# The weight sums of a seven-product down projection: one moved from a DMA to VectorE, another to the second pass, and two units of weights prepared before the last convolution

## The chip, the cores and the metric

One core of a Trainium2 chip runs the whole layer. The metric is the device time of one execution in microseconds (us). The kernel before was timed three times: 950.35 us is the median, 949.29 the lowest and 952.23 the highest. One execution was also profiled; its trace is what the text reads.

## The reference

The program is one layer of a diffusion backbone over 512 tokens of width 1024: a token mixer (spatial gating and gated linear attention) and then a channel mixer. The change lies in the last product of the channel mixer, with the two halves of the up projection called `a` and `val`:

```python
a, val = _split(h @ w_up, (D_FF, D_FF))                      # D_FF = 2816
img = a.reshape(bsz, rows, length // rows, D_FF)
a = lax.conv_general_dilated(img, conv_w[:, :, None, :], (1, 1), 'SAME', ...) + conv_b   # 3 x 3, depthwise
return (jax.nn.gelu(a.reshape(bsz, length, D_FF), approximate=False) * val) @ w_down     # (512, 2816) @ (2816, 1024)
```

The result is scaled by `g2x`, added to the residual stream, and normalised.

## The kernel before, in words

**Up projection and convolution.** The 2816 channels are 22 tiles of 128, numbered by `f`. For each `f` TensorE makes two products of 24 matmuls each (`pa` for `a`, `pv` for `val`, both 128 channels x 512 tokens). Every fp32 operand is split into a high and a low part, so that a product is three matmuls per tile of the contraction: `wh`/`wl` are the parts of a weight, `h2h`/`h2l` those of the activations. ScalarE casts the high part (L183 or L1247), VectorE subtracts it for the low part (L184 or L1248). `conv_part` then copies `pa` out of PSUM on ScalarE (L1193), starts the accumulator `cacc` on ScalarE (L1195), adds the other eight taps on VectorE (L1201), applies gelu on ScalarE (L1202) and multiplies by `pv` on VectorE (L1203). That last multiplication is what frees the PSUM bank of `pv`. After every second `f` four half-width operations on VectorE (L1184 to L1187, `token_sums`) build the sums of token halves.

**Down projection.** Two channel tiles make a pair `p` (0 to 10). The product is done with seven block products instead of eight, in two passes. The first pass has a unit `x` for each pair (weights `ra`: the 1024 columns of the even tile, the second 512 with the first 512 added to them; 12 matmuls) and, for each group of two pairs, a unit `t3` (weights `b22`) and a unit `t2` (weights `t2`), 12 matmuls each. With two pairs a group is thus 48 matmuls. The second pass has a unit `rb` for each pair and a unit `t4` for each group, whose weights are the tile `t2` again with one more addend. Activations are split too: `e` and `s` in the first pass (`eh`, `el`, `sh`, `sl` in the trace), `o` and `s` in the second (L270 on ScalarE, L271 on VectorE). Matmuls of the down projection are L1297. They add up in eight PSUM banks: `p1` and `p5` in pool `gl`, `p7` and `p6` in pool `mm`. The two banks of `p6`, the accumulators of `t2`, are the banks that held `pa` and `pv` of the last `f`.

**Weight sums.** Three kinds of sum over blocks of `w_down` are made by accumulating DMAs that GpSimd issues (`accum_op=ALU.add`, queue q0): a block that already lies in SBUF gets another block of HBM added to it, 256 KB each. L1230 does it for the second half of `ra`, L1225 for `b22`, L1275 for `t2` once unit `t2` has split it. A fourth sum, `t2 = ra[0] + b22`, is VectorE's (L1261).

**What sets the order.** `d_raw` issues the plain load of a tile from SyncE (L1228 for `ra` and `rb`, 512 KB; L1224 for `b22`, 256 KB), and `d_load` does so in the order `ra` 0, `b22` 0, `ra` 1, and so on. `ra`, `rb` and the up projection's weights share one ring of four buffers named `raw`, so a load waits until the tile four places earlier has been read by its last reader; for an `ra` that is the sum L1261 and the split. `wh` and `wl` have rings of five. `b22`, `t2`, `e`, `s`, `o`, the convolution's tiles and `h2` come from one pool of 44 buffers (`heap`). A unit is prepared (`prep`) two units ahead of its matmuls (`LEAD = 2`); a scheduling layer then puts all instructions into one queue per engine, each of which runs strictly in order.

Of the kernel before, what the change touches and what calls it, by code (L numbers as in the profile page):

```python
# [13 lines left out]
ALU = mybir.AluOpType  # L14
# [9 lines left out]
FT = 22  # L24
# [9 lines left out]
def backbone_kernel(  # L34
# [7 lines left out]
    V, A, G, T = nc.vector, nc.scalar, nc.gpsimd, nc.tensor  # L42
# [18 lines left out]
    def late(shape, dt=F32, s="l"):  # L61
        return lp.tile(shape, dt, tag="l", name=nm(s))
# [103 lines left out]
    def stream_load(upto):  # L166
        while pos[0] < min(upto, len(specs)):
            i = pos[0]
            ap, kn, n = specs[i]
            raw = wp.tile([P, kn, n], F32, tag="raw", name=nm("raw"), bufs=4)  # L170
            dma(raw, ap)
            raws[i] = raw
            pos[0] += 1

    def stream_split(upto):
        while pos[1] < min(upto, len(specs)):
            i = pos[1]
            stream_load(i + 1)
            _, kn, n = specs[i]
            raw = raws.pop(i)  # L180
            wh = wp.tile([P, kn, n], F32R, tag="wh", name=nm("wh"))
            wl = wp.tile([P, kn, n], F32R, tag="wl", name=nm("wl"))
            A.copy(wh, raw)  # L183
            V.tensor_tensor(wl, raw, wh.bitcast(F32), op=ALU.subtract)  # L184
            splits[i] = (wh, wl)
            pos[1] += 1

    def weights():
        i = pos[2]
        pos[2] += 1  # L190
        stream_split(i + 2)
        stream_load(i + 1 + AHEAD)
        return splits.pop(i)
# [86 lines left out]
    def prod_cm(ps, w, acts, c0=0, n=512):  # L280
        for k in range(KT):
            prod_k(ps, w, acts, k, c0, n)
# [356 lines left out]
    for d in range(2):  # L639
        t_ = late([P, 4, P], s="pmask")  # L640
# [472 lines left out]
    for t in range(4):  # L1113
        row = []
        for hf in range(2):
            t_ = late([P, 512], s="x1")
# [73 lines left out]
    def conv_part(f, pa, pv):  # L1190
        wcol = lambda tap: ccol[:, tap * FT + f:tap * FT + f + 1]
        a_ = heap([P, 8, GW], s="ca")
        A.copy(a_, pa)  # L1193
        acc = heap([P, 8, GW], s="cacc")
        A.activation(acc, pa, AF.Identity, bias=ccol[:, 198 + f:199 + f], scale=wcol(4))  # L1195
        for tap in (0, 1, 2, 3, 5, 6, 7, 8):
            dy, dx = tap // 3 - 1, tap % 3 - 1
            r0, r1 = max(0, -dy), 8 - max(0, dy)
            c0, c1 = max(0, -dx), GW - max(0, dx)
            o = acc[:, r0:r1, c0:c1]  # L1200
            V.scalar_tensor_tensor(o, a_[:, r0 + dy:r1 + dy, c0 + dx:c1 + dx], wcol(tap), o, op0=ALU.mult, op1=ALU.add)  # L1201
        A.activation(acc, acc, AF.Gelu)  # L1202
        V.tensor_tensor(acc, acc, pv.rearrange("p (r w) -> p r w", w=GW), op=ALU.mult)  # L1203
        gact.append(acc)
        if f % 2:
            token_sums(f // 2)
# [9 lines left out]
    NP = FT // 2  # L1216
    wd = ffn_w_down[0]
    tokens = lambda k: wd[k * P:(k + 1) * P, :]
    dloads, dq = [], {}

    def d_raw(kind, p):
        if kind == "b22":
            t_ = heap([P, 512], s="b22")
            dma(t_, tokens(2 * p + 1)[:, 512:])  # L1224
            G.dma_start(t_, tokens(2 * p)[:, 512:], accum_op=ALU.add)  # L1225
        else:
            t_ = wp.tile([P, 2, 512], F32, tag="raw", name=nm("raw"), bufs=4)
            dma(t_, tokens(2 * p + (kind == "rb")).rearrange("p (a c) -> p a c", c=512))  # L1228
            if kind == "ra":
                G.dma_start(t_[:, 1, :], tokens(2 * p)[:, :512], accum_op=ALU.add)  # L1230
        dq[kind, p] = t_

    for p in range(NP):
# [4 lines left out]
    def d_load(upto):  # L1238
        while dpos[0] < min(upto, len(dloads)):
            d_raw(*dloads[dpos[0]])  # L1240
            dpos[0] += 1

    def d_pair():
        return tuple(wp.tile([P, 2, 512], F32R, tag=tag, name=nm(tag)) for tag in ("wh", "wl"))

    def split_into(wh, wl, raw):
        A.copy(wh, raw)  # L1247
        V.tensor_tensor(wl, raw, wh.bitcast(F32), op=ALU.subtract)  # L1248

    t2, ops = {}, {}  # L1250

    def x_prep(p):

        d_load(2 * p + 7)
        ra, b22 = dq.pop(("ra", p)), dq["b22", p]
        t2[p] = heap([P, 512], s="t2")
        w = d_pair()
        split_into(*w, ra)
        e = split_act(flat(gact[2 * p]), s="e", eng=A.copy)
        s = split_act(s12[p].rearrange("p a c -> p (a c)"), s="s", eng=A.copy)  # L1260
        V.tensor_tensor(t2[p], ra[:, 0, :], b22, op=ALU.add)  # L1261
        ops["a11", p] = [z[:, :256] for z in e]
        ops["s3", p] = [z[:, 256:] for z in e]
        ops["s1", p] = [z[:, :256] for z in s]
        ops["s2", p] = [z[:, 256:] for z in s]
        return w

    def t_prep(kind, ps_):

        w = d_pair()  # L1270
        for j, p in enumerate(ps_):
            src = dq.pop(("b22", p)) if kind == "t3" else t2[p]
            split_into(w[0][:, j, :], w[1][:, j, :], src)
            if kind == "t2":
                G.dma_start(t2[p], tokens(2 * p + 1)[:, :512], accum_op=ALU.add)  # L1275
        return w

    def rb_prep(p):

        d_load(2 * NP + p + 3)  # L1280
        rb = dq.pop(("rb", p))
        w = d_pair()
        split_into(*w, rb)
        o = split_act(flat(gact[2 * p + 1]), s="o", eng=A.copy)
        ops["a12", p] = [z[:, :256] for z in o]
        ops["a22", p] = [z[:, 256:] for z in o]
        if p % 2 == 0:
            n = min(2, NP - p) * 256
            s = split_act(s4[p // 2].rearrange("p a c -> p (a c)")[:, :n], n=n, s="s", eng=A.copy)
            for j in range(n // 256):  # L1290
                ops["s4", p + j] = [z[:, j * 256:(j + 1) * 256] for z in s]
        return w
# [14 lines left out]
    units += [("rb", (p,)) for p in range(groups[-2][0], NP)] + [("t4", g) for g in groups[-2:]]  # L1307
    TAIL = groups[-2][0]
    tw = {}

    def prep(i):
        if i < len(units):
            kind, g = units[i]
            tw[i] = x_prep(g[0]) if kind == "x" else rb_prep(g[0]) if kind == "rb" else t_prep(kind, g)

    for f in range(2, FT):
        pa = mm()
        prod_cm(pa, weights(), h2)
        pv = mm()
        prod_cm(pv, weights(), h2)  # L1320
        if f == FT - 1:
            d_load(7)
        conv_part(f, pa, pv)


# [41 lines left out]
    bank = {}  # L1367
    for name, pool in (("p1", gl), ("p5", gl), ("p7", mm), ("p6", mm)):
        bank[name] = [pool() for _ in range(2)]
    LEAD = 2  # L1370

    def steps_x(i, only=None):
        kind, g = units[i]
# [14 lines left out]
                for t in range(2):  # L1388
                    down(bank[name][t], ops[act, p], t, tw[i], jj if j is None else j, False, True, again=True)

    for i in range(LEAD):
        prep(i)
    for i in range(NX - 3):
        prep(i + LEAD)
        steps_x(i)
        if i == 8:
            for hf in range(2):
                t_ = late([P, 512], s="fng")
# [5 lines left out]
    for i in (x_, t3_, t2_):  # L1404
        prep(i + LEAD)
    steps_x(x_, "p1")
# [25 lines left out]
    for i in range(NX + 2, MAIN):  # L1432
        prep(i + LEAD)
        steps_r(i)
    for i in range(MAIN + LEAD, len(units)):
        prep(i)
# [53 lines left out]
```

## Time and profile before

| what | value |
|---|---|
| median of 3 runs | 950.35 us |
| profiled execution: its time / its span | 950.39 us / 948.7 us |
| mean granted TensorE clock | 0.996 |
| busy share of the span: PE / PEld / DVE / ACT / POOL | 97% / 81% / 74% / 41% / 4% |
| first matmul of the down projection | 828.06 us |
| first matmul of the second pass | 895.08 us |

Times in the trace count from the start of the span. PE is TensorE's matmuls, PEld its weight loads, DVE VectorE, ACT ScalarE, POOL GpSimd, and SPq and POOLq are the queues in which SyncE and GpSimd issue DMAs. A row of the timeline gives the start, the duration, the engine, the line, the operation, output<-input, and in brackets how long the engine sat idle before it and what ended that.

### The profile page before, as it was taken

The page shows a single profiled execution, that of the slowest core. Times are in us where ns is not written, and L with a number is a line of the kernel's source. Part 1 is how long each engine was busy: PE and PEld are TensorE (multiplying, and loading weights), DVE is VectorE, ACT ScalarE, POOL GpSimd, SP SyncE. Part 2 cuts the span into 40 slices and gives each one's busy share as a digit, 9 for nine tenths or more (in the row PEclk, how much of TensorE's full clock was granted, in tenths as well). Part 3 has the DMA queues.
Part 4 walks back from the last instruction along what each step waited for, and adds up shares of the span by engine and source line. Part 5 has one row for each costly group of instructions (what it writes and reads, how often), then busy time and mean ns, then how long its engine had stood idle before and what let it go on. Part 6 is the DMA issues. An engine that isn't in the chain of part 4 may idle for free.

```text
span 948.7 us, 12645 instructions
## 1 busy us (share of the span) xinstructions
PE 921.0 (97%) x4735; PEld 770.2 (81%) x4735; DVE 702.0 (74%) x1248; ACT 390.5 (41%) x669; POOL 42.0 (4%) x67
## 2 busy tenths in 40 slices
PE   6999999999999999999999999999999999999996
PEld 5676898988888888888878888988888888877785
DVE  5557768788699655597664447798888788877897
ACT  5146546567443222223222225543333333445674
POOL 3000000000000000000000000000000001143100
PEclk9999999999999999999999999999999999999999
DMA  9940311132047463683432352333333335599632
GB/s 276 341 129 27 112 46 48 42 112 68 19 137 222 142 206 118 188 277 112 133 111 92 109 182 68 102 98 100 100 88 99 102 90 136 102 259 240 172 111 89
DMA packets 150666, 123.50 MB, mean 130 GB/s; under 512 B 6553, under 2 KB 124645, under 8 KB 150605
## 3 DMA queue, kind: packets, MB, share of 16 engines
q1 hardware_dynamic: 143773, 112.61, 39.1%
q0 software_dynamic: 5104, 8.87, 5.4%
q10 hardware_dynamic: 1728, 1.22, 0.4%
q8 instruction: 37, 0.61, 0.3%
q14 instruction: 24, 0.20, 0.1%
HBM read 120.58 MB, written 2.10 MB: 129 GB/s over the span
## 4 chain that ended last, share of the span: by engine, by line
PE 81%; DVE 7%; DMA 5%; issue 2%; SPq 2%; ACT 2%; POOL 0%; DVEq 0%; POOLq 0%; ACTq 0%
PE mm L278 53%; PE mm L304 5%; PE gl L1297 4%; PE gl L738 3%; PE mm L297 3%; PE mm L1297 3%; DMA raw<-in_ffn_w_down_dram 2%; PE mm L289 1%; PE mm L528 1%; PE gl L304 1%; SPq L215 1%; DMA wa<-in_w_ada_dram 1%; PE mm L842 1%; DVE bc L706 1%; DMA b<-in_ffn_w_down_dram 1%
## 5 line engine op out<-in xcount | busy, mean ns | idle before, releaser
L183 ACT CAST wh<-raw 128x1024 fp32r<-128x1024 f32 x118 | 124.0, 1052 | 303.6 <-PE mm L278 237.4
L184 DVE TENSOR_TENSOR wl<-raw,wh 128x1024 fp32r<-128x1024 f32 x118 | 143.9, 1221 | 76.1 <-ACT wh L183 75.7
L278 PE MATMUL mm<-h2h,wh 128*128 128x512 f32 (+1 forms) x352 | 133.6, 380 | 0.0
L278 PE MATMUL mm<-h2l,wh 128*128 128x512 f32 (+1 forms) x352 | 133.6, 380 | 0.0
L278 PE MATMUL mm<-h2h,wl 128*128 128x512 f32 (+1 forms) x352 | 133.6, 380 | 0.0
L1201 DVE SCALAR_TENSOR_TENSOR cacc<-ca,ccol,cacc 128x441 f32<-128x441 f32 (+2 forms) x176 | 121.8, 695 | 6.7 <-ACT cacc L1195 2.5
L278 PE MATMUL mm<-hxh,wh 128*128 128x512 f32 x296 | 116.5, 394 | 0.0
L278 PE MATMUL mm<-hxh,wl 128*128 128x512 f32 x296 | 115.8, 391 | 0.0
L278 PE MATMUL mm<-hxl,wh 128*128 128x512 f32 x296 | 115.5, 390 | 0.0
L278 PEld LDWEIGHTS mm<-h2h,wl 128*128 128x128 f32 x352 | 66.2, 188 | 12.5
L278 PEld LDWEIGHTS mm<-h2h,wh 128*128 128x128 f32 x352 | 66.2, 188 | 12.5
L278 PEld LDWEIGHTS mm<-h2l,wh 128*128 128x128 f32 x352 | 66.2, 188 | 12.2
L278 PEld LDWEIGHTS mm<-hxh,wl 128*128 128x128 f32 x296 | 55.6, 188 | 11.7 <-issue 0.2
L278 PEld LDWEIGHTS mm<-hxh,wh 128*128 128x128 f32 x296 | 55.6, 188 | 11.6 <-issue 0.5
L278 PEld LDWEIGHTS mm<-hxl,wh 128*128 128x128 f32 x296 | 55.6, 188 | 11.2 <-issue 0.2
L1005 DVE SCALAR_TENSOR_TENSOR acc<-wa,cs,acc 128x512 f32<-128x512 f32 x64 | 45.8, 747 | 4.9 <-DMA wa<-in_w_ada_dram 4.9
L1202 ACT ACTIVATE cacc<-cacc 128x512 f32<-128x512 f32 x22 | 13.9, 633 | 51.1 <-DVE cacc L1201 51.1
L1247 ACT CAST wh<-raw 128x1024 fp32r<-128x1024 f32 x22 | 23.1, 1051 | 28.0 <-issue 13.1
L1230 POOL DMA_DIRECT2D raw<-in_ffn_w_down_dram x11 | 10.1, 919 | 464.6 <-DVE s L1187 432.7
L1248 DVE TENSOR_TENSOR wl<-raw,wh 128x1024 fp32r<-128x1024 f32 x22 | 26.8, 1223 | 0.5 <-ACT wh L1247 0.3
L278 PE MATMUL mm<-obh,wl 128*128 128x512 f32 x64 | 25.0, 390 | 0.0
L278 PE MATMUL mm<-obl,wh 128*128 128x512 f32 x64 | 24.9, 390 | 0.0
(415 smaller groups left out, 1946.1 us busy)
## 6 DMA issues: line engine op xcount, KB each, us to landing
raw<-in_w_in_dram SPq DMA_DIRECT2D x54, 512.0 KB, 3.8
wa<-in_w_ada_dram SPq DMA_DIRECT2D x96, 256.0 KB, 5.2
raw<-in_ffn_w_up_dram SPq DMA_DIRECT2D x44, 512.0 KB, 3.8
raw<-in_ffn_w_down_dram SPq DMA_DIRECT2D x22, 512.0 KB, 5.3
raw<-in_w_br_a_dram SPq DMA_DIRECT2D x8, 512.0 KB, 4.5
raw<-in_w_br_b_dram SPq DMA_DIRECT2D x8, 512.0 KB, 4.3
raw<-in_w_o_dram SPq DMA_DIRECT2D x8, 512.0 KB, 3.4
raw<-in_ffn_w_down_dram POOLq DMA_DIRECT2D x11, 256.0 KB, 7.0
```

What stands on the lines that cost most here:

```text
L183: A.copy(wh, raw)
L184: V.tensor_tensor(wl, raw, wh.bitcast(F32), op=ALU.subtract)
L278: T.matmul(ps, a[:, k, :], b[:, c0:c0 + n], start=(k == 0 and i == 0), stop=(k == KT - 1 and i == 2))
L297: T.matmul(ps, a[:, t * P:(t + 1) * P], b[:, k % 4, :], start=(k == 0 and i == 0), stop=(k == KT - 1 and i == 2))
L304: T.matmul(ps, a[:, t * P:(t + 1) * P], b[:, k % 2, :], start=(k == 0 and i == 0), stop=(k == KT - 1 and i == 2))
L738: T.matmul(ps, p_, q_, start=(start and z == 0), stop=(stop and z == 2))
L1005: V.scalar_tensor_tensor(acc[j], w_, cs[:, k, 0:1], acc[j], op0=ALU.mult, op1=ALU.add)
L1201: V.scalar_tensor_tensor(o, a_[:, r0 + dy:r1 + dy, c0 + dx:c1 + dx], wcol(tap), o, op0=ALU.mult, op1=ALU.add)
L1202: A.activation(acc, acc, AF.Gelu)
L1247: A.copy(wh, raw)
L1248: V.tensor_tensor(wl, raw, wh.bitcast(F32), op=ALU.subtract)
L1297: T.matmul(ps, a[:, t * P:(t + 1) * P], w[b][:, j, c0:c0 + n], start=(first and i == 0), stop=(last and i == 2), skip_group_check=again)
```

## The change

There are four edits. The accumulating DMA on the second half of `ra` (L1230) goes, and `x_prep` does the same sum with one VectorE operation in place, 128 x 512 (L1256 after). The accumulating DMA on `t2` is no longer issued by `t_prep` right after the split for unit `t2`, but by a helper `t4_sums`, called in `rb_prep`, thus in the text of the second pass. The first two units are prepared before `conv_part` of the last `f` (21) instead of after it. The first four loads (`ra` 0, `b22` 0, `ra` 1, `b22` 1) are asked for one `f` earlier.

```diff
@@ d_raw @@
             t_ = wp.tile([P, 2, 512], F32, tag="raw", name=nm("raw"), bufs=4)
             dma(t_, tokens(2 * p + (kind == "rb")).rearrange("p (a c) -> p a c", c=512))
-            if kind == "ra":
-                G.dma_start(t_[:, 1, :], tokens(2 * p)[:, :512], accum_op=ALU.add)
@@ x_prep @@
         w = d_pair()
+        V.tensor_tensor(ra[:, 1, :], ra[:, 1, :], ra[:, 0, :], op=ALU.add)
         split_into(*w, ra)
@@ t_prep @@
             split_into(w[0][:, j, :], w[1][:, j, :], src)
-            if kind == "t2":
-                G.dma_start(t2[p], tokens(2 * p + 1)[:, :512], accum_op=ALU.add)
         return w
 
+    t4_pos = [0]
+
+    def t4_sums(upto):
+        while t4_pos[0] < min(upto, NP):
+            p = t4_pos[0]
+            G.dma_start(t2[p], tokens(2 * p + 1)[:, :512], accum_op=ALU.add)
+            t4_pos[0] += 1
+
     def rb_prep(p):
 
         d_load(2 * NP + p + 3)
+        t4_sums(p + 4)
         rb = dq.pop(("rb", p))
@@ the loop over f @@
         prod_cm(pv, weights(), h2)
+        if f == FT - 2:
+            d_load(4)
         if f == FT - 1:
             d_load(7)
+            for i in range(LEAD):
+                prep(i)
         conv_part(f, pa, pv)
```

What this does to the queues shows in the order of the built programs. The first place is VectorE's queue during the convolutions of `f` 18 (`cacc_7186`) and 19 (`cacc_7262`), where the last weights of the up projection (`wl_7312`, `wl_7365`) are split; `raw_7344` and `raw_7417` are `ra` of pairs 1 and 2, a minus is the order before, a plus the order now:

```order
+L1256 TENSOR_TENSOR raw_7344<-raw_7344 128x512
 L1201 SCALAR_TENSOR_TENSOR cacc_7186<-ca_7184,ccol,cacc_7186 128x7x63
+L184 TENSOR_TENSOR wl_7312<-raw_7234,wh_7311 128x1024
 L1201 SCALAR_TENSOR_TENSOR cacc_7186<-ca_7184,ccol,cacc_7186 128x448
-L184 TENSOR_TENSOR wl_7312<-raw_7234,wh_7311 128x1024
 L1201 SCALAR_TENSOR_TENSOR cacc_7186<-ca_7184,ccol,cacc_7186 128x7x63
 L1203 TENSOR_TENSOR cacc_7186<-cacc_7186,mm_7153 128x512
-L184 TENSOR_TENSOR wl_7355<-raw_7284,wh_7354 128x1024
+L1256 TENSOR_TENSOR raw_7417<-raw_7417 128x512
+L184 TENSOR_TENSOR wl_7365<-raw_7284,wh_7364 128x1024
```

Each new sum stands in the strict order ahead of a split of up-projection weights and of the taps that follow. The sum waits for its `ra` to land, and an `ra` can be loaded only when the split of an earlier up weight has freed its buffer.

The second place is ScalarE's queue around the copies of the last `f` (21), which are `ca_7428` before and `ca_7459` now. Before, they stood behind gelu of `f` 20 (`cacc_7341`) alone:

```order
L1202 ACTIVATE cacc_7341<-cacc_7341 128x512
L1193 COPY ca_7428<-mm_7353 128x512
L1195 ACTIVATE cacc_7430<-mm_7353,ccol 128x512
L270 CAST eh_7462<-cacc_5830 128x512
L270 CAST sh_7466<-s_1152_5856 128x512
```

Now three casts of the down projection stand between gelu of `f` 20 (`cacc_7351`) and them, `t_1367_7424` being `t2` of pair 0:

```order
L1202 ACTIVATE cacc_7351<-cacc_7351 128x512
L1245 CAST wh_7506<-t_1367_7424 128x512
L270 CAST eh_7450<-cacc_5926 128x512
L270 CAST sh_7454<-s_1174_6014 128x512
L1193 COPY ca_7459<-mm_7363 128x512
L1195 ACTIVATE cacc_7461<-mm_7363,ccol 128x512
```

Further back in the same queue gelu of `f` 21 (`cacc_7461`), which stood ahead of the casts of `b22` of pairs 2 and 3, now follows them (`b_1365_7419` and `b_1374_7439`):

```order
L1245 CAST wh_7588<-b_1365_7419 128x512
L1245 CAST wh_7588<-b_1374_7439 128x512
L270 CAST sh_7571<-s_1217_6329 128x512
L1245 CAST wh_7606<-t_1401_7529 128x512
L1202 ACTIVATE cacc_7461<-cacc_7461 128x512
```

The copies of the last convolution thus moved behind the preparation of unit 1, and its gelu behind that of unit `t3` of the second group. `ca_7459` also takes the buffer of `cacc_5926`, which is free only after VectorE has made `el` of pair 1 from it.

The third place is GpSimd's queue of accumulating DMAs at the start of the down projection (`b` is `b22`, `t` is `t2`). Before:

```order
L1225 DMA b_1386_7471<-in_ffn_w_down_dram 128x512
L1275 DMA t_1379_7457<-in_ffn_w_down_dram 128x512
L1230 DMA raw_7474<-in_ffn_w_down_dram 128x512
L1225 DMA b_1399_7529<-in_ffn_w_down_dram 128x512
L1275 DMA t_1388_7477<-in_ffn_w_down_dram 128x512
L1230 DMA raw_7532<-in_ffn_w_down_dram 128x512
```

And now, from `t2` of pair 0 and `b22` of pair 3 (`b_1374_7439`) on:

```order
L1280 DMA t_1367_7424<-in_ffn_w_down_dram 128x512
L1225 DMA b_1374_7439<-in_ffn_w_down_dram 128x512
L1280 DMA t_1376_7444<-in_ffn_w_down_dram 128x512
L1225 DMA b_1399_7524<-in_ffn_w_down_dram 128x512
L1225 DMA b_1408_7556<-in_ffn_w_down_dram 128x512
L1225 DMA b_1421_7624<-in_ffn_w_down_dram 128x512
L1280 DMA t_1401_7529<-in_ffn_w_down_dram 128x512
```

The eleven DMAs on `raw` are gone. Those on `t2` stand only a little later than they did, still among those on `b22` of the first pass, although their call was moved to the second.

More of the change, by code (lines that the diff above doesn't have):

```diff
@@ L1309, in backbone_kernel @@
     tw = {}
+    LEAD = 2
     def prep(i):
@@ L1369, in backbone_kernel @@
         bank[name] = [pool() for _ in range(2)]
-    LEAD = 2
     def steps_x(i, only=None):
@@ L1389, in steps_r @@
                     down(bank[name][t], ops[act, p], t, tw[i], jj if j is None else j, False, True, again=True)
-    for i in range(LEAD):
-        prep(i)
     for i in range(NX - 3):
```

## The prediction

> **What bounds the kernel now.** The split by stage comes first. Its columns are the stretch, its length, the busy time of each engine with the number of instructions, TensorE's granted clock, the DMA engines' busy share and what they moved:
>
> ```profile
> core 0: us, PE busy (x) PEld busy (x) DVE busy (x) ACT busy (x) POOL busy (x), PEclk, DMA share, GB/s
> 828.00:843.00 15.00, 15.00 (x67) 12.24 (x66) 13.71 (x23) 8.01 (x13) 5.25 (x7) 1.00 0.95 225
> 843.00:852.00 9.00, 7.62 (x30) 5.34 (x30) 4.71 (x7) 4.80 (x9) 3.27 (x5) 1.00 1.09 282
> 852.00:877.00 25.00, 24.99 (x111) 20.31 (x109) 18.79 (x28) 12.12 (x20) 10.67 (x13) 1.00 1.05 238
> 877.00:884.00 7.00, 4.94 (x14) 3.68 (x15) 4.33 (x6) 6.07 (x11) 0.00 (x0) 0.76 0.97 255
> 884.00:895.00 11.00, 11.00 (x48) 8.63 (x47) 10.21 (x15) 6.27 (x10) 2.58 (x3) 1.00 0.54 118
> 895.00:940.00 45.00, 45.00 (x204) 37.41 (x203) 42.30 (x66) 28.39 (x50) 0.00 (x0) 1.00 0.29 95
> ```
>
> TensorE is the bound nearly everywhere. It stands still only inside the first pass of the down projection, in 843 to 852 and 877 to 884, and there the DMA share is about 1 while VectorE has room. The timeline of TensorE says what that costs; these are the first matmul of the pass, the last before the first gap (the 66th), every matmul behind a gap, the first at the old pace after the first gap, two slow ones, and the first of the second pass:
>
> ```profile
> 828.06 0.39 PE L1297 MATMUL gl<-wh,eh 128*128 128x512 f32 x1
> ...
> 842.80 0.39 PE L1297 MATMUL gl<-wh,el 128*128 128x512 f32 x1
> 844.06 0.50 PE L1297 MATMUL gl<-wh,sh 128*128 128x512 f32 x1 [0.87 <-ACT sh L270]
> ...
> 845.82 0.39 PE L1297 MATMUL mm<-wh,eh 128*128 128x512 f32 x1
> ...
> 850.34 0.50 PE L1297 MATMUL mm<-wh,sh 128*128 128x512 f32 x1 [0.28 <-ACT wh L1247]
> 851.07 0.50 PE L1297 MATMUL mm<-wl,sh 128*128 128x512 f32 x1 [0.22 <-DVE wl L1248]
> ...
> 877.49 0.50 PE L1297 MATMUL gl<-wh,eh 128*128 128x512 f32 x1 [0.50 <-ACT wh L1247]
> 879.56 0.50 PE L1297 MATMUL gl<-wl,eh 128*128 128x512 f32 x1 [1.57 <-DVE wl L1248]
> ...
> 882.40 0.63 PE L1297 MATMUL gl<-wh,sl 128*128 128x512 f32 x1
> 882.83 0.63 PE L1297 MATMUL gl<-wh,sh 128*128 128x512 f32 x1
> ...
> 895.08 0.39 PE L1297 MATMUL gl<-wh,oh 128*128 128x512 f32 x1
> ```
>
> Without a gap a matmul takes (842.80 - 828.06) / 65 = 0.2268 us. The pass has 24 matmuls for each of 11 pairs, 264, so 59.9 us; it takes 895.08 - 828.06 = 67.0 us. **7.2 us are lost**, and nothing beyond 895 can be won from weights, since PE is full there. From 842.80 to 845.82 lie seven matmuls (1.6 us) in 3.0 us: a gap shown as 0.87 costs 1.4, the slow restart included. Counted the same way the gaps at 850 and 851 add 1.1, those around 878 the other 4.7, about 1.4 of it because the matmuls from 880 to 883 come at 0.43 us each under a granted clock of 0.76.
>
> Behind the gaps stand weights that came late. A cast of `ra` and the sum L1261, which waits for `b22`, say so:
>
> ```profile
> 842.44 1.05 ACT L1247 CAST wh<-raw 128x1024 fp32r<-128x1024 f32 x1 [2.96 <-DMA raw<-in_ffn_w_down_dram]
> ```
>
> ```profile
> 872.28 0.69 DVE L1261 TENSOR_TENSOR t<-raw,b 128x512 f32<-128x512 f32 x1 [4.43 <-DMA b<-in_ffn_w_down_dram]
> ```
>
> The DMA queues of 803 to 895 us (packets, MB, share of the 16 engines) tell what fills them, q0 being the accumulating DMAs and q1 the plain loads:
>
> ```profile
> q0 software_dynamic: 4409, 8.02, 50.8%
> q1 hardware_dynamic: 3620, 9.78, 31.4%
> ```
>
> q0 is 8.02 / 0.262 = 31 DMAs in 0.508 x 92 = 46.7 us, 1.5 us of all engines each; q1 needs 28.9 us for 9.78 MB, 1.55 us for an `ra` and 0.8 for a `b22`. Per pair the first pass needs 1.55 + 0.8 + 3 x 1.5 = 6.9 us of DMA where TensorE needs 24 x 0.2268 = 5.4. DMA is the bound of this pass.
>
> **The change, part by part.** *The sum on `ra`.* One of three accumulating DMAs per pair goes: 6.9 falls to 5.4 us, equal to TensorE's need, with four `ra` loaded before the pass begins, and an `ra` is ready one transfer earlier. VectorE gets 11 operations of 128 x 512. Its prices are steps from start to start in these rows:
>
> ```profile
> 791.10 1.22 DVE L184 TENSOR_TENSOR wl<-raw,wh 128x1024 fp32r<-128x1024 f32 x1
> 792.24 5.10 DVE L1201 SCALAR_TENSOR_TENSOR cacc<-ca,ccol,cacc 128x441 f32<-128x441 f32 x7
> 797.25 1.22 DVE L184 TENSOR_TENSOR wl<-raw,wh 128x1024 fp32r<-128x1024 f32 x1
> 798.39 0.68 DVE L1201 SCALAR_TENSOR_TENSOR cacc<-ca,ccol,cacc 128x441 f32<-128x441 f32 x1
> 799.82 0.69 DVE L1203 TENSOR_TENSOR cacc<-cacc,mm 128x512 f32<-128x512 f32 x1 [0.76 <-ACT cacc L1202]
> 801.92 1.23 DVE L184 TENSOR_TENSOR wl<-raw,wh 128x1024 fp32r<-128x1024 f32 x1 [1.42 <-ACT wh L183]
> ...
> 812.87 1.22 DVE L1248 TENSOR_TENSOR wl<-raw,wh 128x1024 fp32r<-128x1024 f32 x1
> 814.00 5.82 DVE L1201 SCALAR_TENSOR_TENSOR cacc<-ca,ccol,cacc 128x441 f32<-128x441 f32 x8
> ...
> 824.12 0.68 DVE L1201 SCALAR_TENSOR_TENSOR cacc<-ca,ccol,cacc 128x441 f32<-128x441 f32 x1 [2.51 <-ACT cacc L1195]
> 824.72 0.69 DVE L271 TENSOR_TENSOR el<-cacc,eh 128x512 fp32r<-128x512 f32 x1
> ...
> 834.33 0.69 DVE L1203 TENSOR_TENSOR cacc<-cacc,mm 128x512 f32<-128x512 f32 x1
> ```
>
> A wide split is 1.14 us (791.10 to 792.24), a tap behind a tap 0.72, and 0.60 where operations alternate (824.12 to 824.72); the sum takes 0.60. In the steady pass VectorE then has 1.14 + 6 x 0.60 = 4.7 us per pair, under TensorE's 5.4: seven of the sums are hidden by that. If the cover were gone, they would cost 7 x 0.6 = 4.2 us.
>
> *The first sums stand in the convolutions.* They wait for loads. The first `ra` is issued here (SyncE, two issues), and the tile's summary from 765 to 870 gives 3.7 us as the least from issue to landing:
>
> ```profile
> 787.59 5.11 SPq L1228 DMA_DIRECT2D raw<-in_ffn_w_down_dram  x2
> ```
>
> ```profile
> DMA to landing us min/median/max: 3.7/6.6/12.2
> ```
>
> I take 3.7, since the median's loads share the engines with accumulating DMAs that are gone at this place. `ra` 0 lands at 791.3, its sum pushes the split from 791.10 to 791.9; `ra` 1 is issued when that split ends, 793.1, lands at 796.9; its sum and a tap push the next split from 797.25 to 798.1; `ra` 2 is issued at 799.3, lands at 803.0, while VectorE is done with L1203 at 802.1 and waits. The last up weights' split starts at 803.6 instead of 801.92, +1.7 us. TensorE needs it at 828.06 - 24 x 0.2268 = 822.6, so 18 us of slack hide it. The fourth sum makes it +2.3 at the split of 812.87.
>
> *Two units prepared ahead of the last convolution.* Convolution 20 starts behind that split, at 812.87 + 2.3 + 1.14 = 816.3, and has five operations of units 0 to 2 among its eight taps: 13 steps, 8.3 us, to 824.6; L1203 and four more operations of the preparation follow. ScalarE's copies of convolution 21 now stand behind the casts of unit 1 and wait for `el` of pair 1, about 826.6. They take 1.3 us by these rows (the second ends at 824.09):
>
> ```profile
> 822.82 0.59 ACT L1193 COPY ca<-mm 128x512 f32<-128x512 f32 x1 [2.28 <-PE mm L278]
> 823.31 0.78 ACT L1195 ACTIVATE cacc<-mm,ccol 128x512 f32<-128x512 f32 x1
> ```
>
> So the first tap starts at 827.9 instead of 824.12, +3.8. From there L1203 came 10.2 us later (834.33) behind eight taps and eight other operations; now nine others stand there, one more of them wide: 11.35 us, so L1203 runs from 839.25 to 839.95. It frees the bank of `pv`, which is the second bank of `p6`. Before, the 40th matmul was the first to need it, at 836.9, and L1203 was done at 835.0. Now the 48th matmul of the pass needs it, at 828.06 + 47 x 0.2268 = 838.7. **TensorE waits 1.3 us, and 1.7 with a restart of 0.4** as at 844. Bounds: with loads of 5.0 us instead of 3.7 two waits in a row add 2.8, a stall of 4.1; with nothing late it is 0.
>
> Whether that gap costs clock is open: 0.87 at 844 did not, 0.50 and 1.57 within 2.1 us did, for 1.4 us. I take the nearer single gap, no drop. The Trainium skill, page TensorE: Matmul & The Clock Gate, section What's actually happening, has the clock halved only after an idle window of about 3.4 us; by that neither gap of this trace should have cost clock, and the rows of 880 to 883 decide against it. By the page the sum is 944.9, by those rows 946.3.
>
> *`t2` accumulated in the second pass.* In GpSimd's queue these DMAs stay among those of the first pass, so the 5.4 us above still hold one per pair. I count nothing for it: below nothing only in so far as `b22` goes first, above nothing if the second pass were to wait, and that has 45 us at a DMA share of 0.29 for it. *The earlier `d_load`* changes no issue before 803 us, since the ring of `raw` sets those: nothing.
>
> The sum, against the profiled execution (950.39 us, of which 948.7 is the span; the median of 950.35 is the same within 0.04): 950.39 - 7.2 + 1.7 = **944.9 us**.
>
> **The rivals.** *Nothing waits at `p6`*: the sums find their loads early. For it: 1.3 us is the small difference of long chains. 950.39 - 7.2 = 943.2.
>
> *`b22` of pair 3 late.* Its buffer is that of `b22` of pair 0, so its load waits for the sum `t2` of pair 0 (L1261, now L1260), about 824.6; before, nothing of the pass held it. The summaries of L1224 (plain load) and of L1225 (accumulating DMA) are
>
> ```profile
> DMA to landing us min/median/max: 2.5/7.6/9.9
> ```
>
> ```profile
> DMA to landing us min/median/max: 5.0/7.7/12.8
> ```
>
> With DMA idle at 824.6 I take 2.5, then 7.7: 834.8. Its cast on ScalarE stands ahead of gelu 21, and gelu ahead of L1203, so from a landing at 837 on each microsecond goes to TensorE. At 12.8 it lands at 839.9, L1203 ends at 842.9, the gap is 4.2 with 0.4 and 1.4 behind it: 949.2. The page DMA: Bandwidth & Descriptors of the Trainium skill, section Anatomy of one DMA, prices such a DMA at 2.0 us plus its bytes at 436 GB/s, which would be 2.6 us, an estimate, and this rival would not exist; the trace's least of 5.0 speaks against it.
>
> *The slower case is the same place with both legs at their longest*: the load 9.9, the accumulation 12.8, landing at 847.3, L1203 done at 850.3, a gap of 11.6 with 1.8 behind: 956.6. Slower than before begins at a landing of 841.
>
> *DMA stays the bound*, because 5.4 us per pair is no surplus and loads of `rb` begin too. Then the gaps around 878 stay and those of 844 to 851 (2.5) go: 950.39 - 2.5 + 1.7 = 949.6. Against it: four `ra` are ahead, and q0 is 11 x 1.5 = 16.5 us lighter.
>
> **How the numbers follow.** Forecast 0.64 (944.9, with 0.04 of it above 947.5), nothing waits 0.12 (943.2), `b22` late 0.10 (949.2), DMA bound 0.07 (949.6), slower 0.07 (956.6). A measurement of this kernel tells about 0.3%, 2.85 us, from no change. Below 947.5 lie 0.60 + 0.12 = 0.72; within 0.04 + 0.10 + 0.07 = 0.21; above 953.2 0.07. The range goes from 943.0, the floor with nothing lost, to 949.4, which takes in `b22` late and half of the DMA case.
>
> **What would show it.** Right: no gap between 841 and 895; one gap of 0.5 to 3 us about 10.7 us after the first L1303 matmul, ended by L1203; the first tap of convolution 21 about 4 us later than before against the first L1303 matmul; the first pass in 60 to 62 us; about 22 DMAs in q0, DMA share under 1. Wrong: gaps behind casts of `ra` or `b22` as before, or a wait of ScalarE for `b22` of several us ahead of gelu 21; or the wide splits of up weights coming late enough that TensorE waits before 828.

## The result and the profile after

| kernel | median us | runs | against before |
|---|---|---|---|
| before | 950.2 | 6 (949.28 to 952.23) | |
| changed | 944.44 | 6 (943.42 to 946.85) | 0.9941, 95% interval 0.9925 to 0.9957 |

The change saves 5.8 us, and 944.9 had been forecast. The profiled execution, the fastest of the six, took 943.42 us, with a span of 941.7; that is 7.0 us less than the profiled execution of before. Its split by stage, in the columns of before:

```profile
803.00:828.00 25.00, 25.00 (x112) 20.68 (x111) 23.67 (x38) 10.82 (x18) 4.34 (x5) 1.00 0.46 106
828.00:843.00 15.00, 14.45 (x64) 11.67 (x63) 15.00 (x26) 7.40 (x12) 3.99 (x6) 1.00 1.03 245
843.00:852.00 9.00, 9.00 (x42) 7.44 (x41) 9.00 (x15) 6.48 (x10) 2.10 (x4) 1.00 1.06 254
852.00:877.00 25.00, 25.00 (x112) 20.72 (x111) 24.96 (x38) 16.29 (x25) 7.70 (x9) 1.00 0.98 230
877.00:884.00 7.00, 7.00 (x33) 5.79 (x32) 1.92 (x2) 2.65 (x4) 0.86 (x1) 1.00 0.41 101
```

TensorE is full where it stood still before, in 843 to 852 and in 877 to 884, and its clock is 1.00 throughout. The DMA share is still about 1 up to 877, but then it falls to 0.41 where it was 0.97: the transfers are done earlier. VectorE hardly pauses between 828 and 877 and has little left after that. TensorE's timeline, with the first matmul of the first pass, its only gap, and the first matmul of the second pass:

```profile
827.55 0.39 PE L1303 MATMUL gl<-wh,eh 128*128 128x512 f32 x1
...
838.91 0.47 PE L1303 MATMUL mm<-wh,sh 128*128 128x512 f32 x1 [0.55 <-DVE cacc L1203]
...
888.22 0.39 PE L1303 MATMUL gl<-wh,oh 128*128 128x512 f32 x1
```

The pass takes 888.22 - 827.55 = 60.67 us instead of 67.0. That is 0.8 over its 264 x 0.2268 = 59.9, and the gap that L1203 ends accounts for it. So 6.3 of the 7.0 us lie in the pass; 0.5 lie ahead of it. In another execution of the changed kernel (e12) the first matmul of the pass comes at 829.37 us instead of 827.55, so a microsecond or two between whole times can come from ahead of the pass.

### The profile page after: what moved, and what is told of

It reads as the page before. It is cut to its first block, busy times and chain, and to the rows that moved or that the text cites. A ratio compares the mean times of both kernels' runs of the same rounds, so it can differ in the third digit from the quotient of the medians.

```text
span 941.7 us, 12609 instructions
## 1 busy us (share of the span) xinstructions
PE 917.8 (97%) x4735; PEld 769.8 (82%) x4735; DVE 708.0 (75%) x1259; ACT 391.3 (42%) x669; POOL 32.5 (3%) x56
## 4 chain that ended last, share of the span: by engine, by line
PE 86%; DVE 6%; DMA 2%; SPq 2%; ACT 2%; issue 1%; DVEq 0%; ACTq 0%
PE mm L278 55%; PE gl L1303 6%; PE mm L304 5%; PE mm L1303 4%; PE gl L738 3%; PE mm L297 3%; PE mm L289 1%; PE mm L528 1%; PE gl L304 1%; SPq L215 1%; PE mm L842 1%; DVE bc L706 1%; PE gl L769 1%; PE gl L1037 1%; PE gl L528 1%
## 5 line engine op out<-in xcount | busy, mean ns | idle before, releaser
L1225 POOL DMA_DIRECT2D b<-in_ffn_w_down_dram x11 | 9.8, 921 | 468.4 <-DMA b<-in_ffn_w_down_dram 455.2
```

## The experiments

Theory 1 is that of the prediction: the first pass was short of DMA time. Rival A says that DMA time as a sum was no bound and `ra` was late because its load and its accumulation come one after the other. Rival B says that the units prepared ahead bring the gain by themselves. Rival C came later: that VectorE is the new bound. "Loss" below is the length of the first pass in the profiled execution, less 59.9 us. All ratios are against runs of the kernel before on the same chip. e1 to e4, e5 to e8 and e9 to e12 ran on three different chips, on which the kernel before differs by 1 us, so kernels of different sets are compared by their ratios. The loss belongs to the one execution that was profiled; its time was 947.55 us in e3, 951.66 in e5 and 945.25 in e10, up to 3.7 us below the median.

| run | median us | ratio, 95% interval | loss us |
|---|---|---|---|
| before | 949.8 to 950.8 | | 7.1 |
| changed, once more (e12) | 944.65 | 0.9942, 0.9926 to 0.9958 | 0.9 |
| e1 sum on VectorE alone | 943.71 | 0.9936, 0.9923 to 0.9948 | 0.0 |
| e2 units ahead alone | 943.52 | 0.9930, 0.9917 to 0.9942 | 0.1 |
| e3 later call for `t2` alone | 948.65 | 0.9988, 0.9977 to 0.9999 | 4.3 |
| e4 changed, units not ahead | 943.73 | 0.9933, 0.9920 to 0.9945 | 0.0 |
| e5 e1 and scratch DMAs, started by GpSimd | 955.40 | 1.0046, 1.0030 to 1.0062 | 8.8 |
| e6 `t2` really held back | 944.71 | 0.9937, 0.9925 to 0.9950 | 0.3 |
| e7 changed, sums made twice | 949.80 | 0.9989, 0.9977 to 1.0001 | 7.8 |
| e8 `ra` of pair 4 loaded early | 961.80 | 1.0125, 1.0107 to 1.0144 | 1.0 |
| e9 e1 and scratch DMAs, started by ScalarE | 950.90 | 1.0000, 0.9987 to 1.0013 | 5.5 |
| e10 e2, loads held back | 947.33 | 0.9969, 0.9957 to 0.9981 | 2.5 |
| e11 changed, one unit ahead | 944.76 | 0.9941, 0.9926 to 0.9957 | 1.4 |

### The edits one by one: e1 to e4

e1 is the kernel before with the sum alone:

```diff
-            if kind == "ra":
-                G.dma_start(t_[:, 1, :], tokens(2 * p)[:, :512], accum_op=ALU.add)
...
         w = d_pair()
+        V.tensor_tensor(ra[:, 1, :], ra[:, 1, :], ra[:, 0, :], op=ALU.add)
         split_into(*w, ra)
```

> The kernel before with one edit alone: the sum on `ra` is VectorE's. Theory 1 (throughput, the one of the prediction): the first pass of the down projection was bound by the total of DMA, 6.9 us per pair against TensorE's 5.4; one accumulating DMA of 1.5 us less per pair ends that, so all 7.2 us of gaps go: 943.0 us, no gap between 841 and 895, and none at p6 either, because convolution 21 is not delayed. Rival A (latency): DMA as a sum was no bound, but a tile `ra` had to be loaded and then accumulated, one after the other, with four buffers; the accumulation goes here too, so it also says about 943: this run doesn't tell the two apart. Rival B (lead): the gain of the change came from two units prepared earlier: here 948 to 950, with the gaps of 844 to 851 still there.

943.71 us and no gap at all, as theory 1 has it. Two stages of its split:

```profile
828.00:843.00 15.00, 15.00 (x68) 12.43 (x67) 15.00 (x26) 8.66 (x14) 3.38 (x4) 1.00 0.80 200
...
852.00:877.00 25.00, 25.00 (x112) 20.71 (x111) 24.71 (x39) 16.63 (x27) 8.03 (x10) 1.00 1.03 261
```

e2 is the kernel before with the two units ahead and the earlier `d_load`:

```diff
+        if f == FT - 2:
+            d_load(4)
         if f == FT - 1:
             d_load(7)
+            for i in range(LEAD):
+                prep(i)
         conv_part(f, pa, pv)
```

> The kernel before with two edits alone: the first two units prepared ahead of the last convolution, and the first four loads asked for one `f` earlier. All accumulating DMAs as before. Theory 1 and rival A: the weights are as late as before, so the gaps around 878 (4.7 us) stay; those of 844 to 851 (2.5) may go or stay, and L1203 of convolution 21 is later, for up to 1.7 us at p6: 949.4 to 951.9 us. Rival B (lead): 944 to 946.

943.52 us: theory 1 as it stood and rival A both missed, and rival B, 0.5 us above the result, was the nearest. All accumulating DMAs of before are still there, and no gap is left. What moved shows in SyncE's issues. This is the first load that the ring of `raw` lets go on (`ra` of pair 4), first before, then in e2:

```profile
827.86 0.33 SPq L1228 DMA_DIRECT2D raw<-in_ffn_w_down_dram  x1
```

```profile
823.28 0.38 SPq L1228 DMA_DIRECT2D raw<-in_ffn_w_down_dram  x1
```

With the first matmul at 828.06 and at 828.41 it comes 4.9 us earlier against the pass, since the sum `t2` of pair 0 (L1261), the last reader of the buffer, now stands ahead of convolution 21: it starts at 822.10 us instead of 827.11. The split of e2 has the transfers earlier by as much:

```profile
803.00:828.00 25.00, 25.00 (x112) 20.68 (x111) 23.67 (x37) 11.38 (x18) 6.23 (x8) 1.00 0.66 148
828.00:843.00 15.00, 15.00 (x67) 12.27 (x66) 14.88 (x25) 8.70 (x13) 5.38 (x7) 1.00 1.06 267
...
877.00:884.00 7.00, 7.00 (x32) 5.81 (x31) 4.65 (x6) 3.63 (x5) 2.58 (x3) 1.00 0.66 137
```

The share rises from 0.52 to 0.66 in the first row and from 0.95 to 1.06 in the second: 0.14 x 25 + 0.11 x 15 = 5.1 us of transfers done earlier. Before, TensorE waited in all for 0.87 + 0.28 + 0.22 + 0.50 + 1.57 = 3.4 us, and the rest of the 7.1 were restarts and slow matmuls behind the waits. So a head start of 5 us covers the lack. Theory 1 had to be put anew: a balance of DMA time from the moment at which the ring lets the loads go on, not a rate per pair alone.

e3 is the kernel before with the call of `t4_sums` alone:

```diff
             split_into(w[0][:, j, :], w[1][:, j, :], src)
-            if kind == "t2":
-                G.dma_start(t2[p], tokens(2 * p + 1)[:, :512], accum_op=ALU.add)
...
         d_load(2 * NP + p + 3)
+        t4_sums(p + 4)
```

> The kernel before with one edit alone: the accumulation on `t2` issued by the preparation of the second pass. Theory 1: as many DMAs lie in the first pass in GpSimd's queue as before, so nothing: 950.2 us, within 1.5. Rival A (latency): `b22` and `ra` may pass ahead of `t2` in the queue, which would save up to one accumulating DMA's issue per pair, 947 to 949.

It gained 0.12%, with an interval that just leaves out 1. The time lies within rival A's 947 to 949 and 0.05 us below theory 1's range; since the kernel before was at 949.78 us on this chip, 0.4 lower than the 950.2 that the expectation started from, the run doesn't decide between them. The gaps at 844 to 851 are as before; of those around 878 only this one is left, behind which the clock stayed at 1.00:

```profile
878.70 0.50 PE L1304 MATMUL gl<-wl,eh 128*128 128x512 f32 x1 [1.40 <-DVE wl L1248]
```

e4 is the changed kernel with the two units behind the last convolution again:

```diff
-        if f == FT - 2:
-            d_load(4)
         if f == FT - 1:
             d_load(7)
-            for i in range(LEAD):
-                prep(i)
         conv_part(f, pa, pv)
...
+    for i in range(LEAD):
+        prep(i)
     for i in range(NX - 3):
```

> The changed kernel with the two units prepared behind the last convolution again, as before (the sum on VectorE and the later accumulation on `t2` stay). Theory 1: no gap in the first pass and none at p6, since L1203 of convolution 21 comes about 6.3 us after the first matmul of the down projection and not 10.5: the changed kernel's 944.4 less its gap of 0.8 = 943.6 us. Rival B (lead): the weights of the first units are late once more, gaps at 844 to 851 return, 946 or more.

943.73 us and no gap: with the sum on VectorE the units ahead are not needed. The 0.7 us against the changed kernel are about the size of its gap, but the intervals overlap.

### Total or chain: e6, e9, e5

e6 tests theory 1 from the other side. `ra` is loaded and accumulated as before, and the accumulations on `t2` are held back until an `rb` has landed:

```diff
+    def t4_sums(upto, rb):
...
+            g_ = gate[:1, p:p + 1]
+            G.tensor_scalar(g_, rb[:1, 0, :1], 0.0, None, op0=ALU.mult)
+            G.tensor_tensor(t2[p][:1, :1], t2[p][:1, :1], g_, op=ALU.add)
+            G.dma_start(t2[p], tokens(2 * p + 1)[:, :512], accum_op=ALU.add)
```

> The kernel before with one edit alone: the accumulations on `t2` are really held back, each by a one-element operation on GpSimd that waits for the landing of an `rb`, so that none is issued before about 867 us. The sum on `ra` stays an accumulating DMA, and nothing is prepared earlier. Theory 1 (balance of DMA time): 1.5 us per pair less in the first pass up to 867, as with the sum on VectorE: no gap or under 1.5 us of gaps, 943 to 945. Rival A (latency): `ra` of pair 4 is still loaded and then accumulated, the gap at 844 stays, 947 or more. A price could come in the second pass, if an accumulation on `t2` is late for unit `t4`: up to 2 us.

944.71 us. The first four of these DMAs now leave together at the end of the pass:

```profile
875.62 3.29 POOL L1285 DMA_DIRECT2D t<-in_ffn_w_down_dram  x4
```

and TensorE's rows in e6's split are full:

```profile
843.00:852.00 9.00, 9.00 (x40) 7.02 (x39) 6.74 (x10) 5.63 (x9) 3.32 (x4) 1.00 1.08 282
852.00:877.00 25.00, 25.00 (x112) 20.71 (x111) 21.53 (x33) 17.85 (x30) 10.34 (x18) 1.00 0.99 245
877.00:884.00 7.00, 7.00 (x33) 5.79 (x32) 6.80 (x10) 2.17 (x3) 5.03 (x9) 1.00 0.99 162
```

Rival A in its plain form falls here: the load and the accumulation of `ra` were left alone, DMAs that no weight of the first pass waits for were taken out, and the gaps went.

e9 puts the traffic back into e1, without the chain. Each pair gets one more accumulating DMA of 256 KB, into one of two scratch tiles that nobody reads:

```diff
         split_into(*w, ra)
+        z = scr[p % 2]
+        A.copy(z[:1, :1], w[1].bitcast(F32)[:1, 0, :1])
+        G.dma_start(z, tokens(2 * p)[:, :512], accum_op=ALU.add)
```

> As the run before with a scratch accumulation per pair, but the one-element copy that starts each accumulation is ScalarE's and not GpSimd's, whose copy was held for 10 us and with it GpSimd's whole queue. The sum on `ra` is VectorE's, nothing is prepared earlier, the pool of late tiles has one buffer less. Theory 1 (balance of DMA time): 6.9 us of DMA per pair again, so gaps return although no weight waits for the scratch sums, 946 to 950 us, DMA share about 1 up to 884. Rival A (latency of the load and accumulation of one `ra`): 943.7 to 944.5, no gap over 0.5 us.

950.90 us, the time of before, 0.9 above theory 1's range and far from rival A's. In the steady part of the pass ScalarE waits for the casts of `b22`, and TensorE with it:

```profile
857.49 0.62 ACT L1248 CAST wh<-b 128x512 fp32r<-128x512 f32 x1 [3.62 <-DMA b<-in_ffn_w_down_dram]
...
870.38 0.62 ACT L1248 CAST wh<-b 128x512 fp32r<-128x512 f32 x1 [3.75 <-DMA b<-in_ffn_w_down_dram]
```

```profile
852.00:877.00 25.00, 23.19 (x99) 17.92 (x98) 18.82 (x29) 13.09 (x24) 10.74 (x13) 1.00 1.10 268
```

Thirteen matmuls fewer than e1's 112 in these 25 us are about 2.9 us. Not all of the 6.1 us between e1 and e9 (0.64% by the ratios) is traffic: the first scratch DMAs also stand ahead of `b22` in GpSimd's queue, `b22` comes late to convolution 20, and gaps of 0.63 and 0.78 at 834 and 837 follow. The later gaps show what was asked.

One question stays open: whether the limit is the DMA time of both queues together, as theory 1 has it, or the queue of accumulating DMAs by itself (its order and its pace). Every run that lost its gaps has fewer of these DMAs in the pass or starts earlier, and none takes plain loads away alone. For the total speaks that in the kernel before the DMA share is 0.95 or more in every 6 us from 839 to 881, also while GpSimd's queue stood 7.04 us for a load:

```profile
860.97 0.84 POOL L1230 DMA_DIRECT2D raw<-in_ffn_w_down_dram  x1 [7.04 <-DMA raw<-in_ffn_w_down_dram]
```

e5 was the first try at this, with a one-element copy by GpSimd itself:

```diff
-        A.copy(z[:1, :1], w[1].bitcast(F32)[:1, 0, :1])
+        G.tensor_copy(z[:1, :1], w[1].bitcast(F32)[:1, 0, :1])
```

> The kernel with the sum on VectorE alone (943.7 us), and for each pair one more accumulating DMA of 256 KB into a scratch tile that nobody reads, issued once the pair's `ra` has been split; the pool of late tiles has one buffer less, to make room. The traffic of the kernel before, with no weight waiting for it. Theory 1 as the last runs left it (a balance of DMA time: from the moment at which the ring of `raw` lets the loads go on, 6.9 us per pair are too much and 5.4 are not): gaps return behind casts of `ra` or `b22`, 947 to 951 us. Rival A (latency: `ra` was late because its load and its accumulation come one after the other): the chain is as short as with the sum on VectorE, 943.7, no gap.

It can't tell the theories apart, because something else came in between. Two rows of GpSimd show the same copy at two places:

```profile
809.86 0.57 POOL L1262 COPY scr<-wl 1x1 f32<-1x1 f32 x1 [449.86 <-DVE wl L1249]
...
842.23 10.07 POOL L1262 COPY scr<-wl 1x1 f32<-1x1 f32 x1 [2.35 <-DVE wl L1249]
```

The second takes 10 us, with the accumulation on `b22` queued behind it. ScalarE's cast of that `b22` waits for it to land, and this is what TensorE pays (a gap of 5.57):

```profile
859.29 0.62 ACT L1248 CAST wh<-b 128x512 fp32r<-128x512 f32 x1 [8.93 <-DMA b<-in_ffn_w_down_dram]
861.00 0.80 PE L1302 MATMUL gl<-wh,sh 128*128 128x512 f32 x1 [5.57 <-ACT sh L270]
```

### The head start: e10 and e8

e10 is e2 with the loads of `ra` of pairs 4 and 5 held back; the calls that ask for them move behind the split of pair 2:

```diff
+            if kind == "ra" and p in (4, 5):
+                A.copy(t_[:1, 0, :1], gate[0].bitcast(F32)[:1, 0, :1])
             dma(t_, tokens(2 * p + (kind == "rb")).rearrange("p (a c) -> p a c", c=512))
...
-        d_load(2 * p + 7)
+        if p not in (1, 2):
+            d_load(2 * p + 7)
...
+        if p == 2:
+            gate.append(w[0])
+            d_load(2 * p + 7)
```

> The kernel with the two units prepared ahead and all accumulating DMAs as before (943.5 us), but the loads of `ra` of pairs 4 and 5 held back by a one-element copy on ScalarE that waits for the cast of `ra` of pair 2, so that they start at about 829.9 us, 1.5 after the first matmul of the pass instead of 5.1 ahead of it. If the units ahead helped because they let the loads of the ring go on 4.9 us earlier (theory 1, counted from there), 4 us or more are lost again: 947 to 951 us, gaps at 844 to 852. If only the total of DMA time counts, the engines have 7.6 us of other transfers in these 6.6 us (`t2` and `b22` of two pairs), and nothing is lost: 943.5 to 944.5. If the units ahead helped by the work of ScalarE and VectorE that was done earlier (rival B), also 943.5.

947.33 us, 0.39% or 3.7 us over e2 by the ratios; the pass of the profiled execution lost 2.5. SyncE issued the two loads at 829.34, and the gap came late in the pass, not at 844 to 852:

```profile
829.34 1.25 SPq L1232 DMA_DIRECT2D raw<-in_ffn_w_down_dram  x2
```

```profile
873.85 0.50 PE L1305 MATMUL gl<-wl,eh 128*128 128x512 f32 x1 [1.82 <-DVE wl L1252]
```

```profile
803.00:828.00 25.00, 25.00 (x112) 20.71 (x111) 23.51 (x38) 11.11 (x18) 5.74 (x7) 1.00 0.57 122
```

Neither answer fits alone. The engines did carry on with other transfers, so nothing is late at 844; but the share up to 828, in the last row, fell from 0.66 to 0.57, which is 0.09 x 25 = 2.3 us of transfers, about what the pass then lost, near its end. Rival B in its pure form (the earlier work of ScalarE and VectorE is the gain) falls, since that work was done as early as in e2.

e8 is the kernel before with a buffer of its own for `ra` of pair 4, which is asked for ahead of `b22` of pair 3; like e5 and e9 it has one late tile less:

```diff
-            t_ = wp.tile([P, 2, 512], F32, tag="raw", name=nm("raw"), bufs=4)
+            x_ = {"tag": "rawx", "bufs": 1} if (kind, p) == ("ra", 4) else {"tag": "raw", "bufs": 4}
+            t_ = wp.tile([P, 2, 512], F32, name=nm("raw"), **x_)
...
+    dloads[7:9] = [dloads[8], dloads[7]]
```

> The kernel before with one edit alone: `ra` of pair 4 has a buffer of its own and is loaded and accumulated long before the pass; the pool of late tiles has one buffer less, to make room. Nothing is prepared earlier and no sum is moved. Theory 1 (balance of DMA time): 1.55 + 1.5 = 3.1 us of DMA less in the pass, so the gaps of 844 to 851 (2.5 us) go and those around 878 (4.7) shrink as well: 944.5 to 946.5 us. Rival A (latency): only the gap behind `ra` of pair 4 goes, the others stay: 947.5 or more.

Its time, 961.80 us, missed both expectations and says nothing on the pass: the scheduler put the free load to the front of the program (SyncE issues it at 45.12 us, and the DMA share of the first 50 us is 1.05), GpSimd's queue stood 42.8 us for it with other work behind, and TensorE lost 9.9 us in one stretch against before (38.12 busy instead of 47.99):

```profile
50.00:100.00 50.00, 38.12 (x194) 27.53 (x195) 26.39 (x60) 14.85 (x36) 5.76 (x11) 0.85 0.22 56
```

Its first pass by itself has, by the prediction's prices, 3.1 us of DMA less and loses 1.0 us instead of 7.1, in one gap at 897.49. That fits the balance; rival A expected the gaps around 878 to stay.

### VectorE's cover and the gap at p6: e7, e11, e12

e7 makes each sum twice in the changed kernel:

```diff
         V.tensor_tensor(ra[:, 1, :], ra[:, 1, :], ra[:, 0, :], op=ALU.add)
+        V.tensor_tensor(scr, ra[:, 1, :], ra[:, 0, :], op=ALU.add)
```

> The changed kernel with the sum on `ra` made twice on VectorE, the second time into a scratch tile: 0.6 us more VectorE time per pair. Theory 1: VectorE's 4.7 us per pair become 5.3 and stay under TensorE's 5.4; only L1203 of convolution 21 comes later by the sums ahead of it, one to two of them, so the gap at p6 grows by 0.6 to 1.2: 945.0 to 945.6 us. Rival C (VectorE has become the bound, since it is busy for 24.96 of 25 us from 852 to 877): each of the sums of the pass costs its 0.6, 948.5 or more, with gaps behind L1246.

949.80 us, 4.6 over the changed kernel by the ratios, with runs from 945.87 to 952.69. Theory 1's 945.0 to 945.6 missed; rival C's time fits, but not its place. Behind 852 TensorE has no gap, so VectorE did not become the bound of the pass and rival C falls:

```profile
843.00:852.00 9.00, 7.29 (x20) 5.75 (x21) 9.00 (x17) 3.75 (x6) 2.94 (x4) 0.62 0.99 243
852.00:877.00 25.00, 25.00 (x112) 20.70 (x111) 24.26 (x37) 15.46 (x26) 6.55 (x8) 1.00 0.94 216
```

The price is paid at p6, where the wait grew from 0.55 to 4.73 us and cost clock as well: the granted clock was 0.50 from 843.98 to 850.81 us, and the 14 matmuls behind the wait took 6.1 us, 2.9 more than at the usual pace. Together that is 7.6 of the 7.8 us lost:

```profile
844.71 0.77 PE L1305 MATMUL mm<-wh,sh 128*128 128x512 f32 x1 [4.73 <-DVE cacc L1203]
```

VectorE's timeline tells how 0.6 us per sum became that:

```profile
813.06 0.69 DVE L1257 TENSOR_TENSOR raw<-raw 128x512 f32<-128x512 f32 x1 [2.97 <-DMA raw<-in_ffn_w_down_dram]
...
831.93 0.69 DVE L1257 TENSOR_TENSOR raw<-raw 128x512 f32<-128x512 f32 x1 [1.80 <-DMA raw<-in_ffn_w_down_dram]
...
843.88 0.68 DVE L1203 TENSOR_TENSOR cacc<-cacc,mm 128x512 f32<-128x512 f32 x1
```

A scratch sum delays a split, the split frees its buffer later, the next `ra` is loaded later (that of pair 3 by 2.3 us against the first matmul: 806.24 - 827.80 instead of 803.64 - 827.55), and its sum waits for it with the taps of convolutions 20 and 21 queued behind: 2.97 + 1.80 us of waits beside the operations themselves.

e11 is the changed kernel with one unit ahead of convolution 21 instead of two:

```diff
-            for i in range(LEAD):
-                prep(i)
+            prep(0)
         conv_part(f, pa, pv)
...
+    prep(1)
     for i in range(NX - 3):
```

> The changed kernel with one unit prepared ahead of the last convolution instead of two. If the gap at p6 comes from what stands ahead of L1203 of convolution 21 in VectorE's queue, about half of that goes and the gap of 0.8 us with it: 943.6 us, and no other gap. If not, 944.4 with a gap ended by L1203.

944.76 us with a gap ended by L1203, thus the second answer, but the gap is larger than with two units ahead:

```profile
838.48 0.47 PE L1303 MATMUL mm<-wh,sh 128*128 128x512 f32 x1 [1.19 <-DVE cacc L1203]
```

L1203 does start earlier against the first matmul (837.65 - 828.29 = 9.4 us instead of 10.5), but the scheduler has the bank of `pv` needed by the 40th matmul again, as before, and no longer by the 48th: 8 x 0.2268 = 1.8 us earlier. The gap is a difference of the two.

e12 is the changed kernel itself.

> The changed kernel itself once more, beside runs of the kernel before on the same chip as the others of this set: 0.9941 of before, within 0.0015. If one edit alone is as good as the whole change, its ratio lies within the intervals of the sum alone (0.9936) and of the units ahead alone (0.9930).

0.9942, as in the first measurement. The intervals of e1, e2, e4, e6 and e11 all overlap with it: none of these versions beats the changed kernel by more than can be measured.

## Why the prediction was right

*DMA as the bound: right in kind, too narrow in form.* The accumulating DMAs in 803 to 895 are 5.77 / 0.262 = 22 instead of 31:

```profile
q1 hardware_dynamic: 3649, 10.43, 36.9%
q0 software_dynamic: 3168, 5.77, 36.4%
```

e1, e6 and e9 show that taking such DMAs out, those on `ra` or those on `t2`, ends the gaps, and putting others in brings gaps again. The price of a DMA is no constant, though: q0 needs 33.5 us instead of 46.7, 1.5 us each as before, but the plain loads of q1 now need 33.9 us for 10.43 MB, 3.25 us per MB instead of 2.95. The total fell by 8.2 us, not by the 13.2 of q0 alone. What the prediction put as 6.9 against 5.4 us per pair holds only for transfers that begin with the pass. It looked at the loads behind the units ahead only as a risk (`b22` of pair 3 late), and counted their gain at nothing. e2 shows that the units ahead alone take the loss of the pass from 7.1 to 0.1 us, as the sum does in e1. The two don't add, since TensorE alone needs 59.9 us for the pass; the forecast came out because the gain was credited once. Redone from the starts of all 264 matmuls, the loss of before is 7.1 us; 4.2 of it lie around 878, where the prediction has 4.7, and 0.4 in small steps behind 886. With the measured terms its sum is 950.39 - 7.1 + 0.8 = 944.1; that the median came within 0.5 us of 944.9 is in part chance.

*"DMA share under 1" failed.* The loads go on as far as buffers let them, and the share stays at about 1 up to 877, where it falls to 0.41. That fall is no proof of slack by itself: in 877 to 884 the share is 0.56 in e10, which had lost 2.5 us by then, and 0.99 in e6, which had lost 0.3.

*The sums in the pass hidden: right.* No gap follows a sum in the changed kernel, and none in e7 behind 852.

*The first sums in the convolutions: right in place, smaller.* The third sum and the split behind it, the first tap of convolution 21, and its L1203:

```profile
801.78 0.69 DVE L1256 TENSOR_TENSOR raw<-raw 128x512 f32<-128x512 f32 x1 [0.72 <-DMA raw<-in_ffn_w_down_dram]
802.39 1.22 DVE L184 TENSOR_TENSOR wl<-raw,wh 128x1024 fp32r<-128x1024 f32 x1
...
826.74 0.68 DVE L1201 SCALAR_TENSOR_TENSOR cacc<-ca,ccol,cacc 128x441 f32<-128x441 f32 x1
...
838.09 0.68 DVE L1203 TENSOR_TENSOR cacc<-cacc,mm 128x512 f32<-128x512 f32 x1
```

Against the first matmul (828.06 and 827.55) the split is 1.0 us later than before, forecast 1.7; the first tap 3.1, forecast 3.8; L1203 starts 10.5 us behind the first matmul, forecast 11.2. All three come about 0.7 us earlier than forecast, so what was missed at the split seems to run through to the end. The tap is late for the reason forecast, ScalarE's copy waiting for `el` of pair 1:

```profile
825.43 0.59 ACT L1193 COPY ca<-mm 128x512 f32<-128x512 f32 x1 [0.31 <-DVE el L271]
```

*The gap at p6: the right wait, half the size.* Forecast were 1.3 us of wait and 0.4 of restart; the 48th matmul came 0.7 us late (838.91 instead of 827.55 + 47 x 0.2268 = 838.2), and with the restart the pass lost 0.8. This is the mis-sized term of the sum, by the 0.7 us above and the restart. Its upper bound, two waits for loads in a row, is what e7 ran into, there with each sum made twice.

*Rival "`b22` of pair 3 late": its landing right, its cost nothing.* ScalarE's cast and the gelu behind it:

```profile
835.00 0.62 ACT L1245 CAST wh<-b 128x512 fp32r<-128x512 f32 x1 [1.18 <-DMA b<-in_ffn_w_down_dram]
...
837.06 0.63 ACT L1202 ACTIVATE cacc<-cacc 128x512 f32<-128x512 f32 x1 [0.40 <-DVE cacc L1201]
```

It landed at about 835.0, forecast 834.8; against the first matmul that is 7.4 us behind it instead of 6.7. Gelu then still waited for VectorE's last tap. "DMA stays the bound" and the slower case did not come; "nothing waits" is off by the 0.8 us lost in the pass: a gap at p6 is there in all kernels that have both the sum and units ahead (changed, twice, e7 and e11), and in none that has only one of them.

*Clock: no drop, as taken.* The page TensorE: Matmul & The Clock Gate of the Trainium skill, section What's actually happening, has the clock fall after an idle window of about 3.4 us. The single gaps of these runs agree with it: none for 0.55 (changed), 1.40 (e3) and 1.82 us (e10), and a granted clock of 0.50 behind 4.73 us (e7). The drop of before, from 879.95 to 883.37 us behind 0.50 and 1.57 us in close succession, remains outside it: in the 3.42 us ahead of it TensorE was busy for 1.35.

*`t2` in the second pass: nearly nothing, as counted.* e3 has 0.12%. Held back in earnest it brought as much as the whole change (e6, 0.9937). The earlier `d_load` was not tried alone.

## What to carry to other kernels

When a stage is a few us short of transfers, look for when its first transfer may start (which buffer's last reader holds it) as well as for how much it moves: here either one was enough, and doing both gave nothing more. An operation put into a strict queue ahead of other work can cost more than its own time, namely the wait for the load that it reads, and a chain of such waits can grow faster than the sum of the operations, as in e7. A DMA share of 1 alone doesn't prove a bound, and a share that falls doesn't prove slack; look at what ends TensorE's waits, and take transfers out to see whether the waits go.

## What the hardware showed that was not expected

GpSimd's one-element copy in e5 took 0.57 us at 809.86 and 10.07 us at 842.23. In those 10 us VectorE ran 512- and 1024-wide operations with two SBUF inputs back to back. The copy ended at 852.30. VectorE's timeline around that moment:

```profile
851.59 0.68 DVE L271 TENSOR_TENSOR el<-cacc,eh 128x512 fp32r<-128x512 f32 x1
852.34 0.69 DVE L1249 TENSOR_TENSOR wl<-b,wh 128x512 fp32r<-128x512 f32 x1
```

The first of these ends at 852.27, and the 0.07 us up to 852.34 are VectorE's first pause since 842. The page GPSIMD Engine Reference of the Trainium skill, section Key points, says that GpSimd shares its SBUF interfaces with VectorE and contends with such operations. This trace agrees and gives a size: a tiny GpSimd operation was held for 10 us, with all DMAs queued behind it. That VectorE's pause released it was read from these times and not tried by itself. Two later copies fit as well: that of 5.26 us ends at 894.17 in an operation that reads PSUM, that of 2.05 us ends at 880.16, 0.04 us after VectorE fell idle. Two don't: one at 871.44 took 0.43 us beside a VectorE that ran on with two SBUF inputs, and one at 855.30 took 1.78 us while VectorE stood idle. So not every copy is held, and VectorE isn't the only thing that makes one long.
